# The second FFN product of a hybrid decoder block by one level of Strassen's scheme, with its block sums made beside the first product

## The chip, the cores and the metric

The kernel runs on one core of a Trainium2 chip. The metric is the device time of one execution in microseconds (us). Before the change the median of three runs is 2029.3 us (2029.01 to 2032.07). The engines are named as in the profile: PE (TensorE, matrix products; PEld is its weight load), DVE (VectorE), ACT (ScalarE), POOL (GpSimd) and SP (SyncE, whose queue issues nearly all DMAs).

## The reference

A decoder block over 1024 tokens (and 16 learned ones ahead of them) of width 1024: a gated linear recurrence and latent attention side by side, merged by gates, and then a feed-forward part (FFN) of hidden width 2816. All is float32. What matters here is the FFN, its last lines:

```python
u = rms_norm(h, ffn_pre_g[l])
gt, up = jnp.split(u @ w_ffn_in[l], 2, axis=-1)
h = h + rms_norm((jax.nn.silu(gt) * up) @ w_ffn_out[l], ffn_post_g[l])
```

The first product is 1024 x 1024 by 1024 x 5632, the second 1024 x 2816 by 2816 x 1024.

## The kernel before

**Precision.** Every float32 operand of a large product is split into a rounded part `hi` and a remainder `lo` (`split`, L83: one ACT copy, then one DVE subtraction), and a product is three matmuls, hi*hi, hi*lo and lo*hi, added up in PSUM. So a "unit" of 128 x 1024 values costs a DMA load into a tile `wr`, an ACT copy and a DVE subtraction before PE can use it.

**First product (L1081 to 1301).** It already goes by one level of Strassen's scheme (Winograd's form: 7 products of half-size blocks for 8). The hidden width is cut into 22 blocks of 128; block j goes with block j+11, which makes 11 pairs. Each pair takes two chains, one for the gate and one for `up` (class `Chain`, even and odd n). A chain has seven `product(i)` of 4 x 3 = 12 matmuls each, on three PSUM banks: `pa` (two banks) and `pc`. Block sums of the weights are made in place in the `wr` tiles by four DVE instructions (`sums`, L1127 to L1131). After products 2, 3, 7 and 4, `out` (L1154) adds, applies silu, or multiplies the gate by `up`; the results stand in two tiles `sg`, of 128 x 1024 each, four quarters of 128 x 512, and go to DRAM as `act` (L1205, L1211). The order is written in `rest` (L1263): chain n's product 4 comes after chain n+1's product 1. Chains 0 to 3 (`EARLY`) start while the tokens' sums are still being made.

**Second product (L1303 to 1399).** The 22 blocks of `act` and of the weights `wfo` are loaded again and split as units (`second`, L1307), 44 in all, into a ring of 8 pairs of tiles `vh`, `vl`. They are used in groups of two blocks (`GROUP`), four in the last. In each group `out_part` runs over 8 token tiles of 128: two PSUM banks `f2`, for each block and half of the columns three matmuls of 128 x 512 (L1370), and then `add` (L1354): the sums go into the SBUF tiles `acc` by an ACT copy in the first group, by DVE additions later. In the last group each token tile is also squared (ACT, L1356), scaled by `gf` (DVE, L1393), and in `finish` multiplied by the root (made on POOL) and added to `h2` (DVE, L1384), and sent out.

**What sets the order.** The program is written in the order above, and a scheduler then orders each engine's instructions when the kernel is built; each engine works its own list strictly in that order. SP's DMA issues are such a list too: an issue that waits holds up all behind it. Tiles in a ring (`wr`: five; `sg`, `h2` and others: four of tag `io`) are given out again when their last reader is done.

Of the kernel before, what the change touches and what calls it, by code (L numbers as in the profile page):

```python
# [9 lines left out]
F32 = mybir.dt.float32  # L10
# [29 lines left out]
GROUP = 2  # L40
# [7 lines left out]
def block_kernel(ctx: ExitStack, tc: tile.TileContext, a: dict, out: bass.AP, dbg=None):  # L48
# [88 lines left out]
    act_d = dram("act", [NH, P, T])  # L137
# [943 lines left out]
    NP_ = NH // 2  # L1081
# [11 lines left out]
    class Chain:  # L1093
# [87 lines left out]
        def post(self, i):  # L1181
# [4 lines left out]
            elif i == 2:  # L1186
                self.out(0, self.ab[:, 1], self.p1)
            elif i == 5:
# [74 lines left out]
    def rest():  # L1263
        for n in range(EARLY):
# [7 lines left out]
            yield from c.product(6)  # L1272
            yield from c.product(3)
# [6 lines left out]
        for n in range(EARLY, 2 * NP_):  # L1280
# [5 lines left out]
            if n == EARLY:  # L1286
                pE.close()
                wq.append(ctx.enter_context(tc.tile_pool(name="wq2", bufs=1, reuse_waits="tile")))
# [8 lines left out]
            if not last:  # L1297
                chains[n + 1].sums(1)
            yield from c.product(3)
            yield from c.product(7)  # L1300
        yield from chains[-1].product(4)

    ends = list(range(GROUP, NH - 2 * GROUP + 1, GROUP)) + [NH]  # L1303
    groups = [list(range(b, e)) for b, e in zip([0] + ends, ends)]
    held = {}

    def second(j, kind, tiles):  # L1307
        raw = raw_tile()
        SP.dma_start(raw, (act_d if kind == "a" else a["wfo"])[j])
        hi, lo = tiles()  # L1310
        split(hi, lo, raw)
        held[kind, j] = hi, lo

    R = rest()
    steps = 4 * (7 * 2 * NP_ - 2 * EARLY) - 12
    for _ in range(steps):
        next(R)
    second(0, "a", unit_tiles)
    drain(R)
    for kind, j in (("w", 0), ("a", 1)):  # L1320
        second(j, kind, unit_tiles)
# [5 lines left out]
    acc = [gp.tile([P, D], F32, name=f"acc{t}", tag=f"acc{t}") for t in range(NT)]  # L1327

    def ring():
        return [gp.tile([P, 1024], F32R, name=z, tag=z, bufs=8) for z in ("vh", "vl")]  # L1330

    second(1, "w", ring)

    def out_part(gi):
        grp = groups[gi]
        last = gi == len(groups) - 1
        todo = [] if last else [(j, kind) for j in groups[gi + 1] for kind in "aw"]
        if last:
            gf = wide("gf").rearrange("p (a c) -> p a c", a=2)
            SP.dma_start(gf.rearrange("p a c -> p (a c)"), a["ffn_post_g"].partition_broadcast(P))  # L1340
        xs_ = [held.pop(("a", j)) for j in grp]
        ws = [held.pop(("w", j)) for j in grp]
        late = []
        for t in range(NT):
            bs = [bank("f2") for _ in range(2)]
            av = [acc[t][:, 512 * ch : 512 * ch + 512] for ch in range(2)]
            s2 = small("s2", 2) if last else None
            jk = io("jk") if last else None

            def add(ch):  # L1350
                if gi == 0:
                    ACT.copy(av[ch], bs[ch])
                else:
                    DVE.tensor_tensor(out=av[ch], in0=av[ch], in1=bs[ch], op=ALU.add)  # L1354
                if last:
                    ACT.activation(jk[:, 512 * ch : 512 * ch + 512], av[ch], AF.Square, accum_out=s2[:, ch : ch + 1])  # L1356

            for _ in range(2 if len(todo) > 4 or t % 2 == 0 else 0):
                if todo and t < 7:
                    second(*todo.pop(0), ring)  # L1360
            pieces = ((0,), (1,)) if last and t == NT - 1 else ((0, 1),)
            for chs in pieces:
                for i in range(len(grp)):
                    xs = slice(t * P, (t + 1) * P)
                    ahs, als = (z[:, xs] for z in xs_[i])
                    f, l = i == 0, i == len(grp) - 1
                    wh, wl = ws[i]
                    for j, (x, w) in enumerate(((ahs, wh), (ahs, wl), (als, wh))):
                        for ch in chs:
                            PE.matmul(bs[ch], x, w[:, 512 * ch : 512 * ch + 512], start=f and j == 0, stop=l and j == 2)  # L1370
                for ch in chs:
                    add(ch)
            if not last:
                continue
            h2 = io("h2")
            SP.dma_start(h2, h2_d[t])
            ss = small("ss", 1)
            POOL.tensor_tensor(out=ss, in0=s2[:, 0:1], in1=s2[:, 1:2], op=ALU.add)
            r = rstd_of(ss, 1, D)

            def finish(t=t, av=av, h2=h2, r=r):
                for ch in range(2):
                    cc = slice(512 * ch, 512 * ch + 512)
# [93 lines left out]
```

## Time and profile before

| | us |
|---|---|
| median of three runs | 2029.3 |
| the profiled execution | 2030.63 |
| its span, first to last instruction | 2028.5 |
| PE busy in the span | 1982.2 (98%) |
| DVE / ACT / POOL busy | 1144.5 / 662.2 / 126.0 |
| first FFN product in the span | 1340 to 1781 |
| second FFN product and end | 1778 to 2028.5 |

Of the page, part 1 gives each engine's busy time, part 2 the span in 40 slices, part 4 the chain of work that ended last. The views by stretch and by line tell what an engine does in one stage, the DMA view how long a transfer takes from issue to landing. A matmul of 512 columns is shown with 389 ns but they overlap; their pace is read from a run of many.

### The profile page before, as it was taken

The page shows a single profiled execution, that of the slowest core. Times are in us where ns is not written, and L with a number is a line of the kernel's source. Part 1 is how long each engine was busy: PE and PEld are TensorE (multiplying, and loading weights), DVE is VectorE, ACT ScalarE, POOL GpSimd, SP SyncE. Part 2 cuts the span into 40 slices and gives each one's busy share as a digit, 9 for nine tenths or more (in the row PEclk, how much of TensorE's full clock was granted, in tenths as well). Part 3 has the DMA queues.
Part 4 walks back from the last instruction along what each step waited for, and adds up shares of the span by engine and source line. Part 5 has one row for each costly group of instructions (what it writes and reads, how often), then busy time and mean ns, then how long its engine had stood idle before and what let it go on. Part 6 is the DMA issues. An engine that isn't in the chain of part 4 may idle for free.

```text
span 2028.5 us, 26845 instructions
## 1 busy us (share of the span) xinstructions
PE 1982.2 (98%) x10828; PEld 1711.6 (84%) x10828; DVE 1144.5 (56%) x1954; ACT 662.2 (33%) x1130; POOL 126.0 (6%) x178
## 2 busy tenths in 40 slices
PE   7999999999998999999999999989999999999998
PEld 7999898998888988889888888767888888888886
DVE  5455555455443334777773444676655555457666
ACT  5212122112113234555552222553333333341122
POOL 1000000000001100000000000363000000000002
PEclk9999999999999999999999999999999999999999
DMA  4111111011214034111126644652322222233224
GB/s 169 53 42 41 43 42 53 22 53 46 78 67 128 1 109 146 42 48 47 48 72 209 235 149 156 221 183 83 104 104 74 71 104 74 93 135 115 94 84 156
DMA packets 62220, 192.47 MB, mean 95 GB/s; under 512 B 6272, under 2 KB 14976, under 8 KB 62096
## 3 DMA queue, kind: packets, MB, share of 16 engines
q1 hardware_dynamic: 61952, 190.49, 27.9%
q8 instruction: 85, 1.39, 0.3%
q14 instruction: 39, 0.32, 0.1%
q10 hardware_dynamic: 144, 0.26, 0.0%
HBM read 143.55 MB, written 47.19 MB: 94 GB/s over the span
## 4 chain that ended last, share of the span: by engine, by line
PE 91%; DVE 2%; issue 2%; POOL 2%; ACT 1%; DMA 1%; SPq 0%; DVEq 0%; POOLq 0%; ACTq 0%
PE gm L104 26%; PE pa L1150 14%; PE f L1370 10%; PE vb L108 6%; PE pc L1150 6%; PE sb L752 4%; PE fb L104 3%; PE cb L108 3%; PE wo L108 2%; PE ov L813 2%; PE lv L369 2%; PE pT L800 1%; PE fg L104 1%; PE kn L104 1%; PE qn L104 1%
## 5 line engine op out<-in xcount | busy, mean ns | idle before, releaser
L84 ACT CAST wh<-wr 128x1024 fp32r<-128x1024 f32 (+1 forms) x100 | 103.3, 1034 | 326.8 <-issue 146.1
L85 DVE TENSOR_TENSOR wl<-wr,wh 128x1024 fp32r<-128x1024 f32 (+1 forms) x100 | 122.0, 1222 | 121.2 <-ACT wh L84 106.8
L104 PE MATMUL gm<-uh,wh 128*128 128x512 f32 x512 | 164.3, 402 | 0.0
L104 PE MATMUL gm<-uh,wl 128*128 128x512 f32 x512 | 158.3, 390 | 0.0
L104 PE MATMUL gm<-ul,wh 128*128 128x512 f32 x512 | 158.2, 390 | 0.0
L1354 DVE TENSOR_TENSOR acc<-acc,f 128x512 f32<-128x512 f32 x144 | 92.4, 682 | 51.3 <-PE f L1370 50.8
L104 PEld LDWEIGHTS gm<-ul,wh 128*128 128x128 f32 x512 | 96.1, 188 | 20.6
L1107 ACT CAST wh<-wr 128x1024 fp32r<-128x1024 f32 x66 | 69.5, 1053 | 134.5 <-PE pa L1150 78.0
L104 PEld LDWEIGHTS gm<-uh,wl 128*128 128x128 f32 x512 | 95.9, 188 | 20.5
L104 PEld LDWEIGHTS gm<-uh,wh 128*128 128x128 f32 x512 | 92.7, 188 | 16.2
L1370 PE MATMUL f<-vh 128*128 128x512 f32 x320 | 99.2, 389 | 0.0
L1370 PE MATMUL f<-vl,vh 128*128 128x512 f32 x320 | 99.1, 389 | 0.0
L1370 PE MATMUL f<-vh,vl 128*128 128x512 f32 x320 | 99.1, 389 | 0.0
L1108 DVE TENSOR_TENSOR wl<-wr,wh 128x1024 fp32r<-128x1024 f32 x65 | 82.2, 1265 | 25.5 <-ACT wh L1107 25.4
L84 ACT CAST vh<-wr 128x1024 fp32r<-128x1024 f32 x41 | 40.3, 1052 | 146.1 <-PE f L1370 143.2
L372 DVE COPY_PREDICATED AT<-masks,lv 128x128 f32<-128x128 uint8 x192 | 51.5, 322 | 63.9 <-PE lv L369 62.0
L108 PE MATMUL vb<-wh,uh 128*128 128x256 f32 (+1 forms) x288 | 84.3, 293 | 0.0
L108 PE MATMUL vb<-wl,uh 128*128 128x256 f32 (+1 forms) x288 | 81.9, 284 | 0.1
L108 PE MATMUL vb<-wh,ul 128*128 128x256 f32 (+1 forms) x288 | 81.8, 284 | 0.0
L1150 PE MATMUL pa<-xbh,wh 128*128 128x512 f32 x176 | 70.9, 403 | 0.0
L1370 PEld LDWEIGHTS f<-vh 128*128 128x128 f32 x320 | 60.1, 188 | 12.5
L1370 PEld LDWEIGHTS f<-vl,vh 128*128 128x128 f32 x320 | 60.1, 188 | 12.5
(398 smaller groups left out, 5014.2 us busy)
## 6 DMA issues: line engine op xcount, KB each, us to landing
wr<-in_wout SPq DMA_DIRECT2D x24, 512.0 KB, 3.3
wr<-in_wfg SPq DMA_DIRECT2D x24, 512.0 KB, 3.3
wr<-in_wfu SPq DMA_DIRECT2D x24, 512.0 KB, 3.3
wr<-act SPq DMA_DIRECT2D x22, 512.0 KB, 3.4
wr<-in_wfo SPq DMA_DIRECT2D x22, 512.0 KB, 3.4
act<-sg SPq DMA_DIRECT2D x20, 512.0 KB, 2.7
xt<-in_x SPq DMA_DIRECT2D x8, 512.0 KB, 6.4
wr<-in_wv SPq DMA_DIRECT2D x8, 512.0 KB, 3.6
```

The source lines that it names most:

```text
L84: ACT.copy(hi, src)
L85: DVE.tensor_tensor(out=lo, in0=src, in1=_f(hi), op=ALU.subtract)
L104: PE.matmul(o, w, x, start=first and j == 0, stop=last and j == 2)
L108: PE.matmul(o, x, w, start=first and j == 0, stop=last and j == 2)
L369: PE.matmul(b[:, :, c], k[:, cc * P : (cc + 1) * P], qx[:, :, cc], start=True, stop=True)
L372: DVE.copy_predicated(AT[:, 2 * g : 2 * g + 2].rearrange("p c (n w b) -> p (c n) w b", w=2, b=w)[:, :, 1], masks[:, j + s_ + (j > 2)].rear ...
L752: PE.matmul(o, x[:, qs], y[:, b0:e0], start=j == 0, stop=j == 4 and e0 <= d0)
L1107: ACT.copy(hi, src)
L1108: (lo_by or DVE).tensor_tensor(out=lo, in0=src, in1=_f(hi), op=ALU.subtract)
L1150: PE.matmul(o, w[:, k], x[:, k], start=fresh and k == 0 and j == 0, stop=k == HK - 1 and j == 2, skip_group_check=not fresh)
L1354: DVE.tensor_tensor(out=av[ch], in0=av[ch], in1=bs[ch], op=ALU.add)
L1370: PE.matmul(bs[ch], x, w[:, 512 * ch : 512 * ch + 512], start=f and j == 0, stop=l and j == 2)
```

## The change

The second product goes by the same seven-product scheme. Rows are the two token halves (tiles 0 to 3 and 4 to 7), columns the two halves of the width, and the inner dimension is paired as before, block j with j+11. Each of the seven products runs over all 11 pairs in PSUM: 11 pairs x 4 token tiles x 3 = 132 matmuls into four banks, 924 in all, where there were 1056. Products 1, 6, 7 and 4 use the four banks of two tiles `fa`, products 2, 5 and 3 four tiles `fb`; the order is 1, 2, 6, 5, 7, 3, 4, so that one set is read while the other is written. After each product `after_product` copies or adds its four banks into `acc`. The last six pairs of product 4 go token tile by token tile.

The block sums are made while the first product runs. `left_sums` makes four sums of the four quarters of a pair in its two `sg` tiles, in place, once per pair. `right_load` brings the two weight blocks of a pair into two tiles `r0`, `r1`, of which there is one each; `right_sums` makes four sums in them, which go to DRAM as `rt`, `ru`. This is done once per chain in chains 5 to 15. The tiles of `act` go out as `la` (half a tile), `lb`, `lc` and `ld`. A unit of the second product is now half a row of a left and half a row of a right block, two DMAs of 256 KB with rows of 2 KB, and there are 77 of them.

The diff, cut to its core:

```diff
@@ Chain.post
             elif i == 2:
                 self.out(0, self.ab[:, 1], self.p1)
+                if self.up:
+                    SP.dma_start(la_d[self.j], gates[self.j][0][:, :512])
...
-                if self.up:
-                    SP.dma_start(act_d[self.j], gates[self.j][0])
...
                 if self.up:
-                    SP.dma_start(act_d[self.j + NP_], gates.pop(self.j)[1])
+                    SP.dma_start(lb_d[self.j], gates[self.j][1])
+
+    def left_sums(j):
+        s0, s1 = gates.pop(j)
+        (a11, a21), (a12, a22) = ((z[:, :512], z[:, 512:]) for z in (s0, s1))
+        DVE.tensor_tensor(out=a11, in0=a11, in1=a21, op=ALU.subtract)
+        DVE.tensor_tensor(out=a21, in0=a21, in1=a22, op=ALU.add)
+        DVE.tensor_tensor(out=a22, in0=a22, in1=a11, op=ALU.subtract)
+        DVE.tensor_tensor(out=a12, in0=a12, in1=a22, op=ALU.subtract)
+        SP.dma_start(lc_d[j], s0)
+        SP.dma_start(ld_d[j], s1)
...
+    def right_load(j):
+        rights[j] = [wq[1].tile([P, D], F32, name=z, tag=z, bufs=1) for z in ("r0", "r1")]
+        for z, k in zip(rights[j], (j, j + NP_)):
+            SP.dma_start(z, a["wfo"][k])
...
+    def right_sums(j):
...
+        DVE.tensor_tensor(out=b11, in0=b12, in1=b11, op=ALU.subtract)
+        DVE.tensor_tensor(out=b12, in0=b22, in1=b12, op=ALU.subtract)
+        DVE.tensor_tensor(out=b22, in0=b22, in1=b11, op=ALU.subtract)
+        DVE.tensor_tensor(out=b21, in0=b21, in1=b22, op=ALU.subtract)
+        SP.dma_start(rt_d[j], r0)
+        SP.dma_start(ru_d[j], r1)
@@ rest
             if not last:
                 chains[n + 1].load()
+            if 0 <= n - EARLY - 1 < NP_:
+                right_load(n - EARLY - 1)
             yield from c.product(2)
...
                 chains[n + 1].sums(1)
+            if not c.up:
+                left_sums(c.j - 1)
...
             yield from c.product(3)
+            if 0 <= n - EARLY - 1 < NP_:
+                right_sums(n - EARLY - 1)
             yield from c.product(7)
@@ the second product
-    def second(j, kind, tiles):
+    def second(tiles):
+        i, j = todo.pop(0)
         raw = raw_tile()
-        SP.dma_start(raw, (act_d if kind == "a" else a["wfo"])[j])
+        SP.dma_start(raw[:, :512], LEFT2[i][j])
+        SP.dma_start(raw[:, 512:], RIGHT2[i][j])
         hi, lo = tiles()
         split(hi, lo, raw)
...
+    def mul(bs, u, ts, first, last, fresh):
+        hi, lo = u
+        for t in ts:
+            xs = slice(t * P, t * P + P)
+            for j, (x, w) in enumerate(((hi, hi), (hi, lo), (lo, hi))):
+                PE.matmul(bs[t], x[:, xs], w[:, H1], start=fresh and first and j == 0, stop=last and j == 2, skip_group_check=not fresh)
...
-                else:
-                    DVE.tensor_tensor(out=av[ch], in0=av[ch], in1=bs[ch], op=ALU.add)
...
+        else:
+            square(u, H0, b)
+            scale(u, H0, b)
...
+                banks[side] = [bank("fb") for _ in range(4)]
+            else:
+                banks[side] = [z[:, k] for z in (big("fa"), big("fa")) for k in range(2)]
...
+        tail = 6 if i == 4 else 0
+        for j in range(NP_ - tail):
+            while todo and len(held) < AHEAD:
+                second(ring)
+            mul(bs, held.pop(0), range(4), j == 0, j == NP_ - 1, fresh)
...
+        for t in range(4):
+            fetch(t + 4)
+            for j, u in enumerate(held):
+                mul(bs, u, [t], False, j == tail - 1, False)
+            after_product(i, t, bs[t])
```

Here `square` is the ACT instruction at L1386 of the changed kernel, `scale` the DVE one at L1389, and `finish` (L1395) does what it did.

**DVE in one `up` chain of the first product.** In these lists `t` is the tile with the first partial products, `pa` and `pc` the PSUM banks, `wl`/`cl` the remainders of weights and `wr` the raw weights, whose lines 1127 to 1131 are 1128 to 1132 after. Before, from the remainder for product 4 to the result of product 3:

```order
L1108 TENSOR_TENSOR cl<-wr,ch 128x512
L1159 TENSOR_TENSOR t_13403<-t_13403,pa 128x512
L1161 TENSOR_TENSOR sg<-sg,t_13403 128x512
L1108 TENSOR_TENSOR wl<-wr,wh 128x1024
L1127 TENSOR_TENSOR wr<-wr 128x512
L1128 TENSOR_TENSOR wr<-wr 128x512
L1129 TENSOR_TENSOR wr<-wr 128x512
L1131 TENSOR_TENSOR wr<-wr 128x512
L1108 TENSOR_TENSOR wl<-wr,wh 128x1024
L1159 TENSOR_TENSOR t_13403<-t_13403,pc 128x512
```

After, the same stretch of an `up` chain:

```order
L1234 TENSOR_TENSOR r_13658<-r_13658 128x512
L1109 TENSOR_TENSOR cl<-wr,ch 128x512
L1235 TENSOR_TENSOR r_13658<-r_13659,r_13658 128x512
L1160 TENSOR_TENSOR t_13224<-t_13224,pa 128x512
L1109 TENSOR_TENSOR wl<-wr,wh 128x1024
L1162 TENSOR_TENSOR sg<-sg,t_13224 128x512
L1128 TENSOR_TENSOR wr<-wr 128x512
L1236 TENSOR_TENSOR r_13659<-r_13659,r_13658 128x512
L1129 TENSOR_TENSOR wr<-wr 128x512
L1237 TENSOR_TENSOR r_13659<-r_13659 128x512
L1130 TENSOR_TENSOR wr<-wr 128x512
L1132 TENSOR_TENSOR wr<-wr 128x512
```

The four right sums (L1234 to L1237) stand between instructions that empty PSUM and split weights, the first two ahead of the result of product 2.

**SP's issues, about one and a half chains of the first product.** Before, `wr` loads of gate and `up` weights and the two stores of a pair:

```order
L1103 DMA wr<-in_wfu 128x1024
L1103 DMA wr<-in_wfg 128x1024 x2
L1205 DMA act<-sg 128x1024
L1103 DMA wr<-in_wfu 128x1024
L1211 DMA act<-sg 128x1024
L1103 DMA wr<-in_wfu 128x1024
```

After:

```order
L1104 DMA wr<-in_wfg 128x1024
L1238 DMA rt<-r_13522 128x1024
L1239 DMA ru<-r_13523 128x1024
L1229 DMA r_13658<-in_wfo 128x1024
L1104 DMA wr<-in_wfu 128x1024
L1229 DMA r_13659<-in_wfo 128x1024
L1238 DMA rt<-r_13658 128x1024
L1190 DMA la<-sg 128x512
L1229 DMA r_13796<-in_wfo 128x1024
L1239 DMA ru<-r_13659 128x1024
L1104 DMA wr<-in_wfu 128x1024
```

Loads of weights now stand behind stores of sums, and loads of `r0`, `r1` behind the stores that free these tiles.

**PE at the end of the second product.** Before, the last group writes tiles of one bank each; here the step from token tile 6 (`f2_16439`, `f2_16440`) to tile 7:

```order
L1370 MATMUL f2_16439<-vl_16111,vh_16104 128x512
L1370 MATMUL f2_16440<-vl_16111,vh_16104 128x512
L1370 MATMUL f2_16439<-vh_16110,vl_16105 128x512
L1370 MATMUL f2_16440<-vh_16110,vl_16105 128x512
L1370 MATMUL f2_16483<-vh_16010,vh_16004 128x512
```

After, the step from the third token tile of product 4 to the fourth, which are the two banks of one tile `fa_14966`:

```order
L1411 MATMUL fa_14966<-vh_16411,vl_16412 128x512
L1411 MATMUL fa_14966<-vh_16430 128x512
L1411 MATMUL fa_14966<-vl_16431,vh_16430 128x512
L1411 MATMUL fa_14966<-vh_16430,vl_16431 128x512
L1411 MATMUL fa_14966<-vh_16298 128x512
```

The last row here carries a wait for DVE, whose reading of the tile's first bank (L1389) follows the square (L1386). At the step from the first token tile to the second, seven matmuls of the third stand ahead of such a wait.

## Rows read from the trace of the kernel before

**Rows 1.** The page, parts 1 and 2: busy time, and tenths in 40 slices.

```profile
PE 1982.2 (98%) x10828; PEld 1711.6 (84%) x10828; DVE 1144.5 (56%) x1954; ACT 662.2 (33%) x1130; POOL 126.0 (6%) x178
...
PEclk9999999999999999999999999999999999999999
```

**Rows 2.** Stretches of the first product (to 1777) and the second, by engine.

```profile
core 0: us, PE busy (x) PEld busy (x) DVE busy (x) ACT busy (x) POOL busy (x), PEclk, DMA share, GB/s
...
1560.00:1620.00 60.00, 60.00 (x267) 49.67 (x266) 33.04 (x42) 20.76 (x30) 0.00 (x0) 1.00 0.21 71
1620.00:1680.00 60.00, 60.00 (x266) 49.70 (x265) 33.38 (x42) 20.54 (x28) 0.00 (x0) 1.00 0.25 88
...
1777.00:1840.00 63.00, 63.00 (x278) 51.80 (x278) 34.93 (x43) 21.87 (x30) 0.00 (x0) 1.00 0.39 136
1840.00:1900.00 60.00, 60.00 (x267) 49.67 (x266) 41.61 (x56) 11.71 (x12) 0.00 (x0) 1.00 0.32 105
```

**Rows 3.** The chain that ended last: start, us, what, how many.

```profile
1383.48 2.72 PE pc L1150 x12
...
1781.68 205.89 PE f L1370 x908
```

**Rows 4.** Groups by line and shape, 1386 to 1777: busy us, mean ns, idle before.

```profile
L1108 DVE TENSOR_TENSOR wl<-wr,wh 128x1024 fp32r<-128x1024 f32 x60 | 74.5, 1241 | 24.9 <-ACT wh L1107 24.9
...
L1127 DVE TENSOR_TENSOR wr<-wr 128x512 f32<-128x512 f32 x18 | 12.4, 692 | 0.6
```

**Rows 5.** The page, part 5: two groups of the second product.

```profile
L1354 DVE TENSOR_TENSOR acc<-acc,f 128x512 f32<-128x512 f32 x144 | 92.4, 682 | 51.3 <-PE f L1370 50.8
...
L84 ACT CAST vh<-wr 128x1024 fp32r<-128x1024 f32 x41 | 40.3, 1052 | 146.1 <-PE f L1370 143.2
```

**Rows 6.** DMA issues, 1386 to 1777 us: KB each, median us to landing.

```profile
wr<-in_wfg SPq DMA_DIRECT2D x19, 512.0 KB, 3.3
act<-sg SPq DMA_DIRECT2D x19, 512.0 KB, 2.7
```

**Rows 7.** SP's issues in order of time: one issue.

```profile
1603.28 0.33 SPq L1103 DMA_DIRECT2D wr<-in_wfg x1
```

**Rows 8.** DMA, 1055 to 1240 us, a busier stretch.

```profile
DMA packets 10090, 36.31 MB, mean 196 GB/s; under 512 B 1120, under 2 KB 1120, under 8 KB 10080
...
ga<-ga SPq DMA_DIRECT2D x8, 512.0 KB, 4.4
ma<-ga SPq DMA_DIRECT2D x8, 512.0 KB, 3.0
```

**Rows 9.** DMA, 1783.5 to 1799 us, the fill of the ring.

```profile
DMA packets 1279, 4.65 MB, mean 300 GB/s; under 512 B 144, under 2 KB 144, under 8 KB 1278
...
wr<-in_wfo SPq DMA_DIRECT2D x4, 512.0 KB, 5.0
```

**Rows 10.** DMA, the one issue at 1787 to 1788 us.

```profile
wr<-in_wfo SPq DMA_DIRECT2D x1, 512.0 KB, 5.4
```

**Rows 11.** DMA, 790 to 1050 us: transfers with rows of 2 KB.

```profile
ob<-og SPq DMA_DIRECT2D x14, 256.0 KB, 2.0
...
wr<-in_wvv SPq DMA_DIRECT2D x2, 256.0 KB, 2.9
```

**Rows 12.** The end in order of time, PE: start, us, engine, line, what.

```profile
2019.84 0.39 PE L1370 MATMUL f<-vh,vl 128*128 128x512 f32 x1
```

**Rows 13.** The end in order of time, DVE.

```profile
2019.67 1.41 DVE L1384 SCALAR_TENSOR_TENSOR acc<-acc,rs,h 128x512 f32<-128x512 f32 x2
2021.00 0.68 DVE L1354 TENSOR_TENSOR acc<-acc,f 128x512 f32<-128x512 f32 x1
...
2022.46 0.69 DVE L1393 TENSOR_TENSOR acc<-acc,gf 128x512 f32<-128x512 f32 x1 [0.19 <-ACT jk L1356]
```

**Rows 14.** The end in order of time, ACT.

```profile
2021.71 0.63 ACT L1356 ACTIVATE jk<-acc 128x512 f32<-128x512 f32 x1 [1.32 <-DVE acc L1354]
2022.24 0.19 ACT L1356 ACTIVATION_READ_ACCUMULATOR jk<-acc 128x1 f32 x1
```

More of the change, by code (lines that the diff above doesn't have):

```diff
@@ L39 @@
 LEVELS = 7
-GROUP = 2
 def _f(ap):
@@ L136, in block_kernel @@
     n_d = dram("n", [NT // 2, P, D])
-    act_d = dram("act", [NH, P, T])
+    NP_ = NH // 2
+    la_d = dram("la", [NP_, P, 512])
+    lb_d, lc_d, ld_d = (dram(z, [NP_, P, T]) for z in ("lb", "lc", "ld"))
+    rt_d, ru_d = (dram(z, [NP_, P, D]) for z in ("rt", "ru"))
     HW = ((0, 512), (512, 1024))
@@ L1272, in rest @@
             yield from c.product(6)
+            if n == 2:
+                left_sums(0)
             yield from c.product(3)
@@ L1327, in block_kernel @@
     acc = [gp.tile([P, D], F32, name=f"acc{t}", tag=f"acc{t}") for t in range(NT)]
+    AHEAD = 6
     def ring():
[L1330 to L1342, printed above, removed]
-        late = []
[L1344 to L1352, printed above, removed]
-                else:
-                    DVE.tensor_tensor(out=av[ch], in0=av[ch], in1=bs[ch], op=ALU.add)
[L1355 to L1383, printed above, removed]
-                    DVE.scalar_tensor_tensor(out=av[ch], in0=av[ch], scalar=r, in1=h2[:, cc], op0=ALU.mult, op1=ALU.add)
-                    if t == NT - 1:
-                        (SP, ACT)[ch].dma_start(out[t * P : (t + 1) * P, cc], av[ch])
-                if t < NT - 1:
-                    SP.dma_start(out[t * P : (t + 1) * P, :], acc[t])
@@ new lines, in ring, with square, scale @@
+        return [gp.tile([P, 1024], F32R, name=z, tag=z, bufs=AHEAD + 2) for z in ("vh", "vl")]
+    gf = wide("gf")
+    SP.dma_start(gf, a["ffn_post_g"].partition_broadcast(P))
+    H0, H1 = slice(0, 512), slice(512, 1024)
+    sq = gp.tile([P, 32, 2], F32, name="sq", tag="sq")
+    h2t = {}
+    def square(t, cc, src):
+        i = cc.start // 512
+        jk = io("jk")[:, :512]
+        ACT.activation(jk, src, AF.Square, accum_out=sq[:, t, i : i + 1])
+    def scale(t, cc, src):
+        DVE.tensor_tensor(out=acc[t][:, cc], in0=src, in1=gf[:, cc], op=ALU.mult)
@@ new lines, in fetch, with finish @@
+    def fetch(t):
+        h2t[t] = io("h2")
+        SP.dma_start(h2t[t], h2_d[t])
+    def finish(t, parts=1):
+        ss = small("ss", 1)
+        POOL.tensor_tensor(out=ss, in0=sq[:, t, 0:1], in1=sq[:, t, 1:2], op=ALU.add)
+        r = rstd_of(ss, 1, D)
+        h2 = h2t.pop(t)
+        w = D // parts
+        for i in range(parts):
+            cc = slice(i * w, i * w + w)
+            DVE.scalar_tensor_tensor(out=acc[t][:, cc], in0=acc[t][:, cc], scalar=r, in1=h2[:, cc], op0=ALU.mult, op1=ALU.add)
+            (SP, ACT)[i].dma_start(out[t * P : (t + 1) * P, cc], acc[t][:, cc])
@@ new lines, in block_kernel @@
+    banks = {}
+    for i in ORDER:
+        side = i in (2, 5, 3)
+        fresh = i in (1, 2, 5)
+        if fresh:
+            if side:
+                banks[side] = [bank("fb") for _ in range(4)]
+            else:
+                banks[side] = [z[:, k] for z in (big("fa"), big("fa")) for k in range(2)]
+        bs = banks[side]
+        tail = 6 if i == 4 else 0
[3 more added lines that the diff above has]
+            mul(bs, held.pop(0), range(4), j == 0, j == NP_ - 1, fresh)
+            if i == 4 and j < 4:
+                for cc in (H0, H1):
+                    scale(j, cc, acc[j][:, cc])
+                fetch(j)
+                if j:
+                    finish(j - 1)
+        if not tail:
+            for t in range(4):
+                after_product(i, t, bs[t])
+            continue
+        while todo:
+            second(ring)
+        finish(3)
+        late = []
+        for t in range(4):
+            fetch(t + 4)
+            for j, u in enumerate(held):
+                mul(bs, u, [t], False, j == tail - 1, False)
+            after_product(i, t, bs[t])
@@ L1390, in out_part @@
             if late:
                 late.pop()()
-            for ch in range(2):
-                DVE.tensor_tensor(out=av[ch], in0=av[ch], in1=gf[:, ch], op=ALU.mult)
-            late.append(finish)
-        if last:
-            late.pop()()
-    for gi in range(len(groups)):
-        out_part(gi)
+            late.append(lambda t=t: finish(t + 4, 2 if t == 3 else 1))
+        late.pop()()
 def _stationary(w):
```

50 lines of the change are left out of this document (38 added, 12 removed).

## The prediction

> **What bounds the kernel now.** Busy time per engine comes first: PE is busy 98% of the span, at the granted clock of 1.00 in nearly every slice, which is the level of 2.4 GHz [rows 1]. By stretch, PE is busy the whole of each 60 us of the first product and of the second, while DVE has 33 of 60 in the first and 35 to 42 of 60 in the second, ACT 20 and 12 to 22 [rows 2]. No row shows PE waiting in either product, so from 1386 us until the last matmul the time is the number of matmuls times their pace. The chain of waits gives that pace: twelve matmuls of the first product in 2.72 us, 226.7 ns each, and 908 of the second in 205.89 us, 226.7 ns as well [rows 3]. Only the last eight microseconds are another matter: there the end of one tile goes through DVE, ACT, POOL, DVE and a DMA [rows 12 to 14].
>
> **What the change removes from PE.** 1056 matmuls of 128 x 512 become 924 of the same shape, each still with a weight load of its own. 132 x 0.2267 = 29.9 us, all of it on the path. This is the whole gain but for the end; the rest of this part asks what of it is given back.
>
> **The second product beside PE.** A unit now feeds 12 matmuls, 2.72 us of PE. Its split costs ACT 1.05 us [rows 5] and DVE about 1.24 [rows 4], less than half of that each. The 144 additions of 0.682 us, 98 us [rows 5], go; the new ones are a dozen copies on ACT and some 40 DVE instructions of 0.5 to 1.3 us, spread over seven products. Each product writes the banks that the previous one does not use, so its additions lie beside 30 us of matmuls (132 x 0.2267). 77 splits of 1.24 are 95 us, and with the others DVE has about 130 of 210 us: hidden, cost 0. A split is let in when the ring's slot is free, seven units, 19 us, ahead of its use; a load may thus land several microseconds late at no cost. What is at stake is the supply: 77 units of 0.524 MB are 40.4 MB in 924 x 0.2267 = 209.5 us, 193 GB/s against 105 to 136 GB/s now [rows 2]. The fill of the ring shows 300 GB/s for 15 us, with each load 5.0 us under way [rows 9]. It is enough, if half rows move as whole ones do. The nearest rows say so: transfers of 256 KB with rows of 2 KB take 2.0 us to store and 2.9 to load [rows 11], against 2.7 and 3.3 for 512 KB [rows 6]; half the bytes save 0.4 to 0.7 us, so those bytes flow at 370 GB/s or more. I take 0; the other end is the slow rival below.
>
> The Trainium skill, page "DMA: Bandwidth & Descriptors", section Bandwidth, speaks against this step: it asks for transfers of 1 MiB or more and gives a DMA about 2.0 us plus its bytes at 436 GB/s, by which 256 KB get a hundred GB/s when each stands alone. By it alone 154 half loads of 2.6 us, an estimate from that page, would be 400 us, more than the stage has. The trace has loads overlapping.
>
> **The first product beside PE.** DVE gets 44 left and 44 right sums of 0.692 us, the duration of the same kind of sum on weights [rows 4], 61 us over 22 chains. A chain lasts 7 x 2.72 = 19.04 us and DVE is busy 33.2 of 60 us, 10.5 of it, before. Chains 5 to 15 get four right sums (2.8 us), every second one four left sums too: 13.3 or 16.1 of 19.04. It fits, but in a strict order. By the lists, the first right sum stands ahead of the DVE instruction that adds product 2's bank, and it waits for `r0`. What is queued behind it: PSUM evictions and the weight remainders that PE reads one to two products (2.7 to 5.4 us) later.
>
> So the question is whether `r0`, `r1` are there in time. There is one tile of each, so one round must fit in a chain: load r0 and r1 (SP issues 0.33 apart [rows 7]), four sums with other DVE work between them, store them, and only then load the next. With the landings of the first product now, 3.3 for a load and 2.7 for a store [rows 6], and 2.8 of sums, that is 0.33 + 3.3 + 2.8 + 0.33 + 2.7 = 9.5 us. The lists put four to six other DVE instructions of 0.7 to 1.2 us between the sums, about 5 us: 14.5 of 19.04. But the traffic grows: per chain two weight loads, four right transfers and 1.75 of left ones, 7.75 x 0.524 = 4.1 MB in 19.04 us, 213 GB/s instead of 71 to 88 [rows 2]. The stretch that comes nearest moved 196 GB/s, with loads at 4.4 us and stores at 3.0 [rows 8]; that makes the round 15.9 us, 3 to spare. In a burst a load took 5.4 us [rows 10], 1.0 more, and as SP's list waits in turn for stores, one late transfer delays the next. Low end: the round fits in all chains, 0. High end: each of the 11 chains loses the 1.0 us by which 5.4 exceeds 4.4, 11 us. I take 4.0, some 0.4 a chain: nearer the low end, since the row with the like traffic leaves 3 us, but not 0, since SP now has such waits one behind the other and transfers come in clumps. The left sums need no load and their tiles have a chain to spare: 0.
>
> **The end.** Two edits with opposite signs. The last four token tiles are pairs of banks of one tile `fa`, and PE's step to the second bank waits until ACT has squared and DVE has scaled the first. From the rows: a matmul's end 0.16 us past its slot (0.39 - 0.23) [rows 12], about 0.1 to start ACT, 0.63 + 0.19 less the overlap, 0.72, for the square [rows 14], 0.03 and 0.69 for DVE [rows 13], 0.1 back to PE: 1.8 us at the last tile. At the second, seven matmuls (1.6 us) are moved into the gap: 0.2. Together +2.0 (0.2 if a reader of one bank did not hold the other). Against it, the last tile's addition goes. Now PE ends at 20.23 (2019.84 + 0.39), DVE is still at the previous tile until 21.0, adds for 0.68, and ACT squares at 21.71 [rows 12 to 14]. After, ACT reads the bank itself, at about 20.33: -1.4 (0 to -1.5). What follows, POOL, the last multiply and the store, stays.
>
> **The sum.** -29.9 + 0 + 4.0 + 2.0 - 1.4 = -25.3. The profiled execution took 2030.6 (span 2028.5, and 2.1 around it): 2005.3. The median of the runs is 1.3 lower: 2029.3 - 25.3 = 2004.0.
>
> **The rivals.**
> The round fits. Nothing is given back in the first product: -29.3, 2000.0. For it: the 3 us to spare, and the 5.7 us of each chain (19.04 - 13.3) in which DVE would be idle and can swallow a late load. Against: three kinds of transfer in one list.
>
> The round does not fit. SP's waits chain up so that each late store delays the next load, and a chain with both kinds of sums (16.1 us of DVE) has no idle time to recover. Price 1 to 2 us in each of 11 chains, 11 to 22: 2011 to 2022, say 2014. For it: the burst's 5.0 to 5.4 us [rows 9, 10]; against: it lasted 15 us, and 213 GB/s is well under its 300.
>
> The second product starves, the case that ends slower. Rows of 2 KB at half rows' pitch move at half of what whole rows did: 150 instead of 300 GB/s. Then 40.4 MB take 269 us instead of 209.5, +60: 2064. It begins to bite below 193 GB/s, and makes the kernel slower than before below 40.4 / (209.5 + 25.3) = 172. For it: no row shows two half loads in flight for long. Against: the 370 GB/s between sizes worked out above. The skill's rule on sizes has the same sign; by single half loads of 2.9 us in a row [rows 11], 154 x 2.9 = 447 us, it would be 2241, which the overlap of the fill rules out nearly.
>
> That the matmuls are not saved is no rival: the change's list has 924 of them.
>
> **How the numbers follow.** Forecast (4 +- 3 given back, 2001 to 2008): 0.47. The round fits, about 2000: 0.30. It does not fit, 2009 to 2022: 0.16. Starved: 0.05 (0.01 of it the rule's single loads). The last 0.02 for no difference, by a mishap that is not in the rows. Likeliest 2004.0. The range: from 1999, a microsecond under the case that fits, to 2014 in the middle of the case that doesn't; outside are about 0.06 below and 0.13 above. Faster than by 0.2%, 4 us, about what a measurement of this kernel can tell from no change: 0.93; same 0.02; slower 0.05.
>
> **What would show it.** In the changed profile, stretches of the second product show PE busy throughout, 0.2267 us a matmul, DMA near 190 GB/s: the 29.9. If DMA stands at its full share there and PE has gaps, the supply failed. Stretches over chains 5 to 15 show PE busy 60.0 of 60 if the round fits, 58 to 59 by the forecast, with DVE waiting for a DMA of `r0` or `r1` and PE for DVE behind it; the chains after them show no gap. At the end, PE waits once for `acc` by about 1.8 us, and the last matmul is followed by ACT at once. The prediction is wrong if matmuls run at another pace, or if the weight loads of the first product land late because of the stores ahead of them in SP's list.

## The result, and the profile after

The changed kernel takes 2003.3 us (median of four runs, 2001.3 to 2004.4) against 2029.15 (four runs, 2028.7 to 2032.1). The ratio is 0.9868, 95% interval 0.9851 to 0.9885: 25.9 us less, where 25.3 were predicted. The profiled execution took 2004.36 us.

The page of the changed kernel has 132 matmuls less [rows 1]:

```profile
span 2002.5 us, 26882 instructions
PE 1953.7 (98%) x10696; PEld 1685.6 (84%) x10696; DVE 1152.3 (58%) x1936; ACT 697.9 (35%) x1159; POOL 126.7 (6%) x178
```

By stretch, with the columns of [rows 2]:

```profile
1440.00:1500.00 60.00, 59.08 (x261) 48.62 (x260) 42.72 (x61) 21.12 (x30) 0.00 (x0) 1.00 0.79 275
1500.00:1560.00 60.00, 58.26 (x256) 47.58 (x255) 48.20 (x69) 19.12 (x26) 0.00 (x0) 1.00 0.72 246
1560.00:1620.00 60.00, 58.88 (x258) 48.10 (x257) 38.79 (x54) 21.07 (x30) 0.00 (x0) 1.00 0.53 185
1620.00:1680.00 60.00, 60.00 (x266) 49.70 (x265) 38.89 (x51) 19.62 (x27) 0.00 (x0) 1.00 0.30 106
...
1840.00:1900.00 60.00, 60.00 (x266) 49.70 (x265) 29.25 (x26) 25.40 (x27) 0.00 (x0) 1.00 0.63 193
1900.00:1960.00 60.00, 60.00 (x267) 49.69 (x266) 32.23 (x32) 28.21 (x36) 0.00 (x0) 1.00 0.61 194
```

PE is busy throughout the second product but for one wait at its end, at 193 GB/s. In the first it has gaps from 1440 to 1620 us, where DMA moves up to 275 GB/s, and none behind them.

What the gaps cost is best read from one matmul that every chain has: the first of product 5, which writes `pc`. In order of time, in chains 4 and 21, before (L1150) and after (L1151):

```profile
1443.16 0.39 PE L1150 MATMUL pc<-xth,wh 128*128 128x512 f32 x1
...
1766.84 0.39 PE L1150 MATMUL pc<-xth,wh 128*128 128x512 f32 x1
```

```profile
1441.52 0.39 PE L1151 MATMUL pc<-xth,wh 128*128 128x512 f32 x1
...
1770.53 0.39 PE L1151 MATMUL pc<-xth,wh 128*128 128x512 f32 x1
```

That is 323.68 us before, 17 chains of 19.04, and 329.01 after: 5.33 lost, nearly all in chains 6, 7, 9, 10 and 11, of 19.4 to 20.5 us. The busy time of the windows shows only 3.8 of it, since a matmul's 0.39 us hides the first 0.16 of each gap, and the second matmul behind a gap comes after 0.34 us instead of 0.23.

So the two profiled spans, 2028.5 and 2002.5, differ by 26.0 in four pieces:

| piece | before | after | difference |
|---|---|---|---|
| to product 5 of chain 0 | 1383.32 | 1381.68 | -1.64 |
| on to product 5 of chain 21 | 383.52 | 388.85 | +5.33 |
| on to the last matmul | 253.00 | 225.27 | -27.73 |
| to the end of the span | 8.7 | 6.7 | -2.0 |

The end, in order of time; [rows 12 to 14] are its counterpart:

```profile
1991.78 0.51 PE L1411 MATMUL fa<-vh 128*128 128x512 f32 x1 [1.50 <-DVE acc L1389]
...
1995.80 0.39 PE L1411 MATMUL fa<-vh,vl 128*128 128x512 f32 x1
1996.23 0.60 ACT L1386 ACTIVATE jk<-fa 128x512 f32<-128x512 f32 x1 [5.23 <-PE fa L1411]
...
1996.95 0.69 DVE L1389 TENSOR_TENSOR acc<-fa,gf 128x512 f32<-128x512 f32 x1 [3.45 <-ACT jk L1386]
1996.99 0.19 POOL L1397 TENSOR_TENSOR ss<-sq 128x1 f32<-128x1 f32 x1 [4.82 <-ACT jk L1386]
```

### The profile page after: what moved, and what is told of

The parts are those of the page before. It is cut to its first block, busy times and chain, and to the rows that moved or that the text cites. A ratio compares the mean times of both kernels' runs of the same rounds, so it can differ in the third digit from the quotient of the medians.

```text
span 2002.5 us, 26882 instructions
## 1 busy us (share of the span) xinstructions
PE 1953.7 (98%) x10696; PEld 1685.6 (84%) x10696; DVE 1152.3 (58%) x1936; ACT 697.9 (35%) x1159; POOL 126.7 (6%) x178
## 5 line engine op out<-in xcount | busy, mean ns | idle before, releaser
L84 DVE TENSOR_TENSOR vl<-wr,vh 128x1024 fp32r<-128x1024 f32 x74 | 90.0, 1224 | 80.9 <-ACT vh L83 78.2
L103 PEld LDWEIGHTS gm<-ul,wh 128*128 128x128 f32 x512 | 96.1, 188 | 20.5
L83 ACT CAST vh<-wr 128x1024 fp32r<-128x1024 f32 x74 | 77.7, 1054 | 98.2 <-PE fb L1411 46.7
L1151 PE MATMUL pa<-xth,wh 128*128 128x512 f32 x176 | 69.0, 392 | 3.7 <-DVE t L1160 2.8
L1151 PE MATMUL pa<-xbh,wh 128*128 128x512 f32 x176 | 70.3, 399 | 0.0
L1151 PE MATMUL pa<-xbh,wl 128*128 128x512 f32 x176 | 69.8, 397 | 0.0
L1151 PE MATMUL pa<-xbl,wh 128*128 128x512 f32 x176 | 69.6, 396 | 0.0
L1151 PE MATMUL pa<-xtl,wh 128*128 128x512 f32 x176 | 68.5, 389 | 0.0
L1151 PE MATMUL pa<-xth,wl 128*128 128x512 f32 x176 | 68.5, 389 | 0.0
```

The lines of the kernel that those rows point to most:

```text
L83: ACT.copy(hi, src)
L84: DVE.tensor_tensor(out=lo, in0=src, in1=_f(hi), op=ALU.subtract)
L103: PE.matmul(o, w, x, start=first and j == 0, stop=last and j == 2)
L1151: PE.matmul(o, w[:, k], x[:, k], start=fresh and k == 0 and j == 0, stop=k == HK - 1 and j == 2, skip_group_check=not fresh)
```

## The experiments

All in one table. The second column is the median of 4 or 5 runs (one run with *), the third the stretch from product 5 of chain 4 to product 5 of chain 21 less the 323.68 of a stretch without a gap, the fourth from there to the last matmul; the last two are from one profiled execution each.

| kernel | us | lost in the first product | to the last matmul |
|---|---|---|---|
| changed | 2003.3 | 5.33 | 225.27 |
| e7_again (the same) | 2001.6 | 2.75 | 225.25 |
| e4_no_right | 2003.1* | 0.00 | 225.23 |
| e1_paced | 1999.7 | 2.70 | 225.25 |
| e2_pool_sums | 2019.1 | 20.20 | 225.27 |
| e5_late | 2002.4 | 3.05 | 225.21 |
| e12_left_only | 2001.8 | 0.72 | 225.24 |
| e9_late_both | 1998.5 | 0.00 | 225.25 |
| e3_banks | 1999.0 | 1.56 | 222.98 |
| e6_late_banks | 2000.1 | 1.82 | 222.98 |
| e10_all | 1996.4 | 0.00 | 222.98 |
| e8_half_more | 2002.4* | 3.94 | 225.21 |
| e11_twice | 2021.4* | 2.27 | 247.28 |

The times alone can't settle a question of 2 us: the runs of one kernel spread over 1.6 (e9_late_both) to 5.7 us (e12_left_only), and a part of that is decided ahead of the change (last section). The third and fourth column can.

**The changed kernel again.** 

> The changed kernel once more, unaltered. Its first profile lost 5.3 us in the first product and began product 5 of chain 0 at 1381.7; e3_banks, whose lists are the same up to the second product, lost 1.6 and began at 1380.7. Theory A (the loss hangs on when transfers land, so it differs from run to run with the same lists): the stretch is again above 324 but not 329.0; times from 1999 to 2004. Rival (the loss belongs to the lists): 329 +- 0.5 again, and the exchange of banks must have something to do with the first product.

2.75 us lost; e3_banks (1.56), e8_half_more (3.94) and e11_twice (2.27) have the same lists up to the second product. With equal lists the loss goes from 1.6 to 5.3, so the lists alone do not set it, and the rival falls. That the landing of transfers sets it follows from DVE's waits below; no run varied the landings alone.

**Without the right part.** `right_load` and `right_sums` are not called. 

> Change: the right part is left out in the first product (no loads of r0 and r1, no right sums, no stores of rt and ru), and the second product takes raw halves of wfo in their place, so its right operands are not the block sums; the number and size of its loads is the same. It measures what the right part costs altogether. If the 5.3 us lost between product 5 of chain 4 and product 5 of chain 21 (329.0 us, 323.7 without a gap) come from the right part alone, the stretch takes 323.7 to 324 and the kernel 1998; if the left sums and their three more stores have a part in it, the stretch stays above 325. DMA in that stretch falls from 199 to about 115 GB/s.

No gap at all, with the left sums in place:

```profile
1440.00:1690.00 250.00, 250.00 (x1104) 207.01 (x1103) 151.42 (x197) 86.08 (x119) 0.00 (x0) 1.00 0.33 112
```

So the right part, or what its traffic does to others, is the whole loss: five executions with it lost 1.6 to 5.3, this one without it nothing. The single time is no lower since product 5 of chain 0 began at 1385.63 us here, 3.95 later than in the changed kernel.

**What is lost there.** In the changed kernel's waits (who waits for whom: us, times, longest), DVE from 1440 to 1700 us:

```profile
DVE r L1234 <- DMA r<-in_wfo: 16.1, 5, 4.8
...
DVE r L1235 <- DMA r<-in_wfo: 9.1, 8, 1.8
...
DVE sg L1219 <- DMA lb<-sg: 2.1, 3, 1.0
```

One such wait in order of time, DVE and then PE:

```profile
1538.99 0.69 DVE L1234 TENSOR_TENSOR r<-r 128x512 f32<-128x512 f32 x1 [4.33 <-DMA r<-in_wfo]
1539.60 0.69 DVE L1109 TENSOR_TENSOR cl<-wr,ch 128x512 fp32r<-128x512 f32 x1
1541.52 0.69 DVE L1235 TENSOR_TENSOR r<-r,r 128x512 f32<-128x512 f32 x1 [1.24 <-DMA r<-in_wfo]
1542.13 0.68 DVE L1160 TENSOR_TENSOR t<-t,pa 128x512 f32<-128x512 f32 x1
```

```profile
1541.71 0.39 PE L1151 MATMUL pc<-xth,wl 128*128 128x512 f32 x1
1542.86 0.50 PE L1151 MATMUL pa<-xth,wh 128*128 128x512 f32 x1 [0.76 <-DVE t L1160]
```

DVE stands at `r`, 4.33 and 1.24 us; behind it is the addition that reads the bank `pa` (L1160), and PE, due 0.23 after 1541.71, starts its next product in that bank at 1542.86.

One of the four largest gaps stands behind the other kind of wait, for the store `lb`. PE waits for ACT's copy of product 6's bank:

```profile
1488.85 0.50 PE L1151 MATMUL pa<-xth,wh 128*128 128x512 f32 x1 [0.93 <-ACT t L1204]
```

That copy stood behind a cast of weights, and the cast behind DVE's L1219, which began at 1484.65 after 0.99 us of waiting for `lb`. The store itself was issued only at 1480.63, because the multiplication ahead of it (L1162, 1479.92) stood in DVE's list behind a wait of 1.02 us for `r` and three right sums. So this wait, too, comes with the right part: without it L1219 waited 0.4 us for `lb` in all.

And the sums come faster than the prediction had it:

```profile
L1234 DVE TENSOR_TENSOR r<-r x11: 682/691/693, 1449.6 to 1578.8; 128x512 f32<-128x512 f32 x11
```

Eleven rounds begin within 129.2 us, 12.9 apart: three in two chains, from chain 4 on, not one in each of the chains 5 to 15. A round starts as soon as the last one's stores let it: from 1440 to 1600 us the loads of `r` (L1229) wait 22.5 us for these stores.

**One round per chain.** The load waits for a column that POOL writes from the chain's product 1:

```diff
         for z, k in zip(rights[j], (j, j + NP_)):
+            POOL.tensor_tensor(out=z[:, :1], in0=after, in1=after, op=ALU.add)
             SP.dma_start(z, a["wfo"][k])
```

> Change: ahead of each load of r0 and r1, one POOL instruction writes a single column of the tile from the ACT copy of the same chain's product 1. The load must wait for it, so there is one round of the right part (two loads, four sums, two stores) per chain, where the changed kernel's lists pack 11 rounds into 129 us (L1234 from 1449.6 to 1578.8 us, 12.9 us a round). In the changed kernel the stretch from product 5 of chain 4 to product 5 of chain 21 takes 329.0 us, 17 x 19.04 = 323.7 would be without a gap: 5.3 us lost. Theory A, the packing is the cause (a round starts before the stores of the last one have landed, and DVE stands at r with evictions queued behind): the stretch falls to 324 to 325 us, the kernel to about 1998.5 us; DVE's waits for r, 25 us now, fall under 3. Rival B, the strict order on DVE costs some 0.4 us a round at any pace, as the prediction had it: 328 us, no change beyond 1 us. Rival C, the traffic as a whole makes loads late: the bytes are the same but spread over 209 us, so half of the loss stays, 326 us.

Eleven rounds from 1461.8 to 1654.9 us, 210 GB/s where it was 254 (1440 to 1600 us), and still 2.70 lost, in two chains, 6 and 14. DVE still waits for every load, as here with the addition of `pa` behind it:

```profile
1482.45 0.69 DVE L1235 TENSOR_TENSOR r<-r 128x512 f32<-128x512 f32 x1 [3.62 <-DMA r<-in_wfo]
1483.06 0.68 DVE L1165 TENSOR_TENSOR sg<-t,pa 128x512 f32<-128x512 f32 x1
```

The packing is not the cause, at least not alone: the waits for `r` came to 26.3 us here. The stretch of 326.4 lies between A and B and near C's 326, but e7_again shows that the unpaced kernel can lose as little (2.75), so it speaks for none of them. Two pairs of r0 and r1 were not tried.

**The sums on POOL.** `right_sums` on POOL instead of DVE. 

> Change: the four right sums of a pair run on POOL, which has no work in this stretch; loads, stores, bytes and pace stay. Theory A (DVE stands at r, and the evictions queued behind it hold PE): nothing of DVE's list waits for r any more, the stretch from product 5 of chain 4 to product 5 of chain 21 falls from 329.0 to 324 us, the kernel to about 1998.5. Rival C (traffic makes the weight loads themselves late): the stretch stays at 328 to 329 and PE waits for DVE lines that wait for wr. Rival D (POOL and DVE slow each other): the early sums on POOL took 1.29 us alone and up to 2.16, and a DVE remainder beside them 1.67 instead of 0.68 or 2.6 for two instead of 2.4; by it DVE's instructions get longer and 1 to 3 us stay lost.

All missed: 20.2 us lost, the kernel 16 us slower. DVE waits no more for `r`, but for the next transfer in its list. DVE, ACT, PE and POOL around the largest gap:

```profile
1526.61 1.22 DVE L1109 TENSOR_TENSOR wl<-wr,wh 128x1024 fp32r<-128x1024 f32 x1 [0.21 <-ACT wh L1108]
1534.25 0.69 DVE L1219 TENSOR_TENSOR sg<-sg 128x512 f32<-128x512 f32 x1 [6.42 <-DMA lb<-sg]
...
1536.07 1.75 DVE L1129 TENSOR_TENSOR wr<-wr 128x512 f32<-128x512 f32 x1
1537.85 1.63 DVE L1130 TENSOR_TENSOR wr<-wr 128x512 f32<-128x512 f32 x1
```

```profile
1539.59 1.04 ACT L1108 CAST wh<-wr 128x1024 fp32r<-128x1024 f32 x1 [10.58 <-DVE wr L1130]
1540.55 0.58 ACT L1204 COPY t<-pa 128x512 f32<-128x512 f32 x1
```

```profile
1541.18 0.80 PE L1151 MATMUL pa<-xth,wh 128*128 128x512 f32 x1 [7.35 <-ACT t L1204]
```

```profile
1535.52 1.74 POOL L1235 TENSOR_TENSOR r<-r,r 128x512 f32<-128x512 f32 x1 [4.54 <-DMA r<-in_wfo]
1537.35 1.59 POOL L1236 TENSOR_TENSOR r<-r,r 128x512 f32<-128x512 f32 x1
```

The third left sum (L1219) overwrites `sg`, whose store `lb` has not landed. Behind it stand sums of weights; for those ACT's cast waits 10.58 us; behind the cast in ACT's list is the copy of product 6's bank, and PE stands 7.35 us for that. Behind this gap the granted clock was 0.52 from 1541 to 1545 us, where the changed kernel's windows above show 1.00, and seven matmuls came 0.43 us apart, the pace of 1.2 GHz, instead of 0.227; so of the 20.2 us PE's waits are 15.0 and much of the rest is slower matmuls. The sums of weights are also slow, 1.63 to 1.75 us for 0.68, exactly while POOL's sums run, and these take 1.59 to 1.74 for the 1.29 of a sum that runs alone; this is rival D's mechanism, though the largest gap begins with the wait of 6.42 us for `lb`. The Trainium skill, page "SBUF — State Buffer", section "SBUF: two separate sides", says that DVE with two inputs and a reading POOL take turns, one blocked for the other's whole instruction. These rows agree: on either engine the starts come 1.7 to 1.8 us apart, near the 0.68 + 1.29 = 1.97 us of one after the other and far from the 1.29 of both at once.

**The right sums later.** e1_paced, and a POOL instruction that reads `r0` and the copy of product 6 ahead of the sums, so that they come behind the evictions (the first sum overwrites the column that POOL reads, so it has to wait for POOL, and POOL for the copy):

```diff
+    def right_hold(j, after):
+        z = small("hold", 1)
+        POOL.tensor_tensor(out=z, in0=rights[j][0][:, :1], in1=after, op=ALU.add)
...
+                right_hold(n - EARLY - 1, c.u2[:, :1])
```

> Change: one round per chain as in e1_paced, and besides, a POOL instruction that reads one column of r0 and one of the copy of product 6 stands ahead of the four right sums, so that DVE's sums stand some 8 us later, behind the remainders and the eviction of product 2. In e1_paced 2.7 of the 5.3 us were left, in two chains of 20.2 and 20.5 us; at the first of them DVE stood 3.6 us at r (load issued 1476.2, sum at 1482.45, 6.2 us) with the addition of pa queued behind it, and PE waited 0.86. Theory A (what costs is a DVE wait for r ahead of evictions, whatever the pace): DVE waits for r under 2 us in all and no chain is over 19.3 us; stretch from product 5 of chain 4 to product 5 of chain 21 at 323.7 to 324.5, kernel about 1997 to 2000 with the spread of its start. Rival C (any late transfer, of weights or of the sg stores too): 1 to 3 us stay, with PE behind DVE lines that wait for lb or wr.

DVE's waits for `r` are gone altogether, and 3.05 are lost: rival C. The row of e2_pool_sums is there, smaller. DVE, ACT, PE in chain 14:

```profile
1638.82 0.69 DVE L1219 TENSOR_TENSOR sg<-sg 128x512 f32<-128x512 f32 x1 [1.98 <-DMA lb<-sg]
```

```profile
1641.43 1.05 ACT L1108 CAST wh<-wr 128x1024 fp32r<-128x1024 f32 x1 [4.14 <-DVE wr L1130]
1642.39 0.58 ACT L1204 COPY t<-pa 128x512 f32<-128x512 f32 x1
```

```profile
1643.02 0.50 PE L1151 MATMUL pa<-xth,wh 128*128 128x512 f32 x1 [0.91 <-ACT t L1204]
```

**The left sum later as well.** The same kind of instruction ahead of the left sums:

```diff
             if not c.up:
+                z = small("hold", 1)
+                POOL.tensor_tensor(out=z, in0=gates[c.j - 1][1][:, 512:513], in1=c.u2[:, :1], op=ALU.add)
                 left_sums(c.j - 1)
```

> Change: e5_late, and one more POOL instruction ahead of the left sums that reads a column of sg and one of the copy of product 6. In e5_late DVE waited no more for r, but 3.05 us were still lost, and at the loss in chain 14 DVE stood 1.98 us at L1219, which overwrites a tile whose store lb had not landed; behind it were three sums of weights, for which ACT's cast waited 4.1, and behind that cast the copy of product 6's bank, for which PE waited 0.91 of idle time. The third left sum now stands behind that copy, some 5 us later. Theory A (each loss is an in-order engine that waits for a transfer, with an eviction queued behind it; take both such places away and nothing is lost): stretch from product 5 of chain 4 to product 5 of chain 21 at 323.7 to 324.2 us. Rival (DVE is simply too full in a chain with 16 us of 19 of work, and the loss moves on): 325 to 327 again, with PE waiting for a DVE or ACT line that waits for no transfer.

Theory A: every chain takes 19.04 us, at the traffic of the two paced kernels before (207 GB/s from 1440 to 1600 us, where e1_paced had 210 and e5_late 209), and DVE waits for no transfer from 1440 to 1700 us:

```profile
1440.00:1500.00 60.00, 60.00 (x266) 49.73 (x265) 40.83 (x54) 21.74 (x30) 3.82 (x10) 1.00 0.57 207
1500.00:1560.00 60.00, 60.00 (x266) 49.69 (x266) 45.45 (x63) 19.72 (x28) 3.82 (x10) 1.00 0.58 209
```

From 1440 to 1690 us DVE is busy for 178.0 us, and was for 173.9 in the changed kernel, so its load was not the cause. Both kinds of wait for a transfer were, where an eviction stood behind them. How much each edit gives is open: each of them makes the scheduler order the rest of DVE's list anew, and the two added waits together without the pacing were not tried.

**The left one alone.** 

> Change: of the three edits of e9_late_both only the last: the POOL instruction ahead of the third left sum; the right rounds stay packed, three in two chains, and DVE's sums of r where they were. In the changed kernel's trace three of the four larger gaps of PE (0.97, 0.76, 1.07 us idle) stand behind DVE waits for r, one (0.93) behind the wait for lb. Theory A (both kinds of wait cost, each by itself): the gap for lb goes, those for r stay: stretch from product 5 of chain 4 to product 5 of chain 21 at 325.5 to 328, kernel 2000 to 2002. Rival (the wait for lb alone is what delays the rest): 323.7 to 324.3, kernel 1998.5 as e9_late_both.

0.72 lost (324.4), between the two and next to the rival's. The rounds stay packed (1456.7 to 1582.0) and DVE still waits 22.3 us for `r`, but that now costs one gap of PE, of 0.43 us idle. The edit also changed the order of the right sums and the evictions in DVE's list, so how much of the 5.3 belongs to `r` and how much to `lb` isn't settled by it; one profiled execution each, with 1.6 to 5.3 from equal lists, wouldn't settle it either.

**The banks.** `if side:` becomes `if not side:` where the bank sets are allotted. 

> Change: the two bank sets change places, so that products 1, 6, 7 and 4 use four tiles of one bank and products 2, 5 and 3 two tiles of two banks. In the changed kernel PE waits in product 4 for the reader of the neighbouring bank of the same tile, 1.90 us at the last token tile (matmul 1989.88 to 1991.78 less 0.23 = 1.67) and 0.4 at the second. Theory A (the wait belongs to the tile of two banks, not to the bank): both waits go, about 2.0 us, the time falls to about 2001.3, the first product keeps its 5.3 us. Rival B (the banks are not the point, PE waits for ACT and DVE to be done anyway): no change, 2003.3. Rival C (a new wait at the start, as one of the four single banks is still pc of the last chain): what the end gains the start loses, 0 to -1 us.

Theory A: PE has no wait in product 4, and from product 5 of chain 21 to the last matmul it is 222.98 instead of 225.27, 2.29 less; nothing is given back at the start. The median is 4.3 lower than the changed kernel's 2003.3, and 2.6 lower than the 2001.6 of e7_again, the same kernel; the times are no finer than that. The first product lost 1.56 in the profiled execution.

**Both.** 

> Both edits, e5_late and the exchanged bank sets of e3_banks. If the two are independent: stretch of the first product 324 us, last matmul to the end 6.7 us, no wait of PE in product 4; 5.3 + 2.3 = 7.6 us under the changed kernel's 2003.3, 1995.7. If the sum is less, by what the first product keeps.

The banks' part as expected (222.98); the first product kept 1.82, in chain 14, behind L1219 again. 

> The three edits together: e9_late_both and the exchanged bank sets of e3_banks. Expected under theory A: stretch 323.7 to 324.2, no wait of PE in product 4, last matmul about 223 us after product 5 of chain 21 and the end 6.7 us later. Against e7_again's profile (326.4 and 225.3): 2.5 + 2.3 = 4.8 us less, 1996 to 1998 by the median, where the start of the first product gives or takes 2 us.

No loss, 222.98, and 1996.35 us: ratio 0.9843 to the kernel before (0.9828 to 0.9857). Its four runs, 1995.75 to 1997.55, lie under all eight of the changed kernel (1999.86 to 2004.36): the fastest version found.

**The supply of the second product.** One more load per unit, from the fourth unit on, into a tile `xx` that nobody reads:

```diff
         SP.dma_start(raw[:, 512:], RIGHT2[i][j])
+        if gpx:
+            xx = gpx[0].tile([P, 512], F32, name="xx", tag="xx", bufs=3)
+            SP.dma_start(xx, a["wfo"][2 * j][:, :512])
```

> Change: each unit of the second product loads a third half row of 256 KB into a tile that nobody reads, 290 GB/s wanted where the changed kernel has 193. It measures how far the supply is from its end. If transfers of 256 KB are the limit near 200 GB/s (the rival of the prediction: half rows at half the pace of whole ones), PE starves: the second product takes 1.5 times as long, about 2100 us. If half rows move as whole ones do, 300 GB/s as in the fill of the ring before, PE has no gap or a few: 2003 to 2010 us, landings up from 3 to 5 us.

> Change: as in e8_half_more, but the extra load per unit is a whole row of 512 KB that nobody reads: 387 GB/s wanted. With a half row more, 298 GB/s were moved at a DMA share of 0.87 to 0.88 and PE had no gap. By that share the end is near 298 / 0.88 = 340 GB/s: 81 MB would take 238 us instead of 209.5, PE has gaps of about 28 us, 2030 us. Rival: the single loads get slow enough first that the ring of eight runs dry at less, or the share of 0.88 is no limit: 2003 us or over 2060.

The first of these windows is of e8_half_more, the other two of e11_twice:

```profile
1840.00:1900.00 60.00, 60.00 (x266) 49.73 (x265) 30.56 (x27) 25.35 (x27) 0.00 (x0) 1.00 0.87 298
```

```profile
1840.00:1900.00 60.00, 58.70 (x259) 48.18 (x258) 27.19 (x24) 21.61 (x23) 0.00 (x0) 1.00 1.00 382
...
1960.00:2000.00 40.00, 29.90 (x109) 21.11 (x109) 24.51 (x26) 14.37 (x24) 8.30 (x12) 0.85 0.93 334
```

At one and a half times the traffic PE has no gap, with loads of 256 KB landing after 3.5 to 5.3 us. At twice, DMA is full at 382 GB/s, the loads land after 6.3 to 7.8 and PE loses 22.0 us (247.28 - 225.27), not 28. But this is no steady want of data: in the window at 382 GB/s seven matmuls are missing, 1.6 us, while from 1960 to 2000 us 109 passed where 40 us hold 176, so some 15 of the 22 us fall there. SP's list there also has the loads of `h2` and the stores of the output; PE waited 4.82 us ahead of 1990.47 for ACT's split, and the granted clock was 0.50, the level of 1.2 GHz, from 1990 to 2000. The estimate of 28 us came near by another way than its own.

## Why the prediction was right, step by step

**Matmuls, -29.9.** Without PE's wait in product 4 the last piece is 222.98 against 253.00: -30.0. The term holds.

**The second product, 0.** It holds with room: 193 GB/s wanted, no gap at 298. The "slow rival" is out. The rule of the Trainium skill, page "DMA: Bandwidth & Descriptors", section Bandwidth (transfers of 1 MiB or more), does not apply here: it prices a transfer by itself, and with several in flight halves of 256 KB reach what whole rows do [rows 9]. The 2.0 us and 436 GB/s that the prediction took from there are a fit for DMAs issued by GpSimd, in the page's section "Anatomy of one DMA — SWDGE (gpsimd) path"; these go from SP's queue. The section Bandwidth gives 436 GB/s as the ceiling on SBUF's side and about 358 as what binds transfers between HBM and SBUF. The window of 1780 to 1840 us in e11_twice moved 391, so here the second did not bind.

**The first product, +4.0.** 5.3 in the profiled run; 2.8, 3.9, 2.3 and 1.6 with equal lists, mean 3.2. The size is right; the step behind it is right in its mechanism (DVE at `r`, evictions behind) and wrong in three places. "One round must fit in a chain": the lists run three in two chains, which could be counted in DVE's list and wasn't, so the traffic was 275 and 246 GB/s where the step had 213, and the loss sits in five chains from 6 to 11, 0.35 to 1.41 us each, not 0.4 in each of 11. "The left sums need no load and their tiles have a chain to spare: 0": they need a store to have landed, `lb`, issued just ahead; of the four largest gaps of PE one (0.93 us idle, at 1488.85) stands behind that. By themselves the left sums do cost 0 (e4_no_right); beside the right part they do not. And "the 1.0 us by which 5.4 exceeds 4.4" is not the unit: the wait of 4.33 at 1538.99 cost its chain 1.07, one of 1.09 at 1490.71 nothing, by what stood behind them.

**The rivals of that step.** "The round fits" is what e9_late_both shows, with one round per chain and the sums at another place of the list: nothing lost, 1998.5. "The round does not fit" took as its reason that DVE has no idle time to recover in; in e3_banks DVE was busy 49.6 of the 60 us from 1500 on, and PE had no gap there:

```profile
1500.00:1560.00 60.00, 60.00 (x266) 49.58 (x265) 49.58 (x70) 19.84 (x27) 0.00 (x0) 1.00 0.75 268
```

**The end, +2.0 and -1.4.** PE's waits cost 2.29 (e3_banks). The rest came to -2.0, not -1.4: ACT starts 0.43 us after the last matmul's start, as predicted (20.33 - 19.84 = 0.49), and POOL's first instruction behind it took 0.19, where before it was 0.70.

**The sum.** -30.0 + 5.3 + 2.3 - 2.0 = -24.4, and -1.6 from ahead of the change: -26.0 between the spans of the two profiled executions, -25.9 between the medians, -25.3 predicted. The term missing from the sum is the spread of the start, and it is as large as the errors. That the number came so near is in part luck: the 1.3 that the first product lost above its 4.0 and the 1.6 from ahead of the change cancel, and the same kernel gained 27.2 in e7_again (2028.8 to 2001.6).

## What to carry to other kernels

Busy time says whether work fits beside PE; what it costs is decided by order: find each instruction of an in-order engine that waits for a transfer, a store that must land before an overwrite included, and look what stands behind it. Where that is the emptying of a bank, a true dependency that costs nearly nothing (one column, on an idle engine) puts the waiting instruction behind it, and here cost less than moving the work to another engine. When work is said to be done "once per" something, count it in the engine's list.

## What the runs showed of the hardware

**The start of the first product differs from run to run.** Product 5 of chain 0 began between 1379.86 and 1381.68 us in five executions with equal lists up to there, and 1383.32 in the kernel before. The granted clock is one part of it. Windows of 4 us (PE busy, PEclk, DMA share, GB/s), before and then after, whose lists differ:

```profile
1372.00:1376.00 4.00, 1.26 (x5) 0.75 0.53 166
1376.00:1380.00 4.00, 4.00 (x14) 0.50 0.25 96
```

```profile
1372.00:1376.00 4.00, 1.66 (x6) 0.79 0.63 192
1376.00:1380.00 4.00, 4.00 (x19) 0.79 0.18 71
```

After a window in which PE was busy 1.26 of 4 us, the next was granted 0.50, which is 1.2 GHz, for all of its 4 us, and 14 matmuls passed where 19 did in the other run. It differs with equal lists as well: from 1372 to 1376 us e7_again was granted 0.50 and the changed kernel 0.79. What decides between the two was not tried.

**Transfers of 256 KB.** 298 GB/s without a gap, and 382 at a full DMA beside transfers of 512 KB, above.
